# GLA hybrid trunk: the product for v with rows of h as TensorE's weights, and the decays moved one stage on

## The chip, the core and the metric

The program runs on one core of one Trainium2 chip. The time is the device time of one execution in microseconds (us); the median of three runs is compared. The engines are TensorE (PE in the profile, with its weight loads as PEld), VectorE (DVE), ScalarE (ACT), GpSimd (POOL) and SyncE (SP), which issues every DMA.

## What is computed

One layer of a decoder trunk on x of 1024 rows by 1024 columns. Only the parts that the change touches are shown; v has 4 heads of 256 columns, q and k 4 heads of 128.

```python
h = rms_norm(x, norm_mix_g)
proj = einsum('bsd,dc->bsc', h, w_in)
(q, k, v, z_a, gk_low, cb, cc, xc, z_c, g_a, g_c) = split(proj)
gk = log_sigmoid(gk_low @ w_gk2 + b_gk) / 16          # the decays
o = gla_chunked(q, k, v, gk)                          # rows of v by head and chunk
y_a = (rms_norm(o, gla_norm_g) * silu(z_a)) @ w_branch_a
u = causal_dwconv(cc * xc, conv_w)
y_c = ((cb * u) * silu(z_c)) @ w_branch_c
merged = sigmoid(g_a + b_ga) * y_a + sigmoid(g_c + b_gc) * y_c
x = x + merged @ w_out                                # then the per-layer embedding and a last norm
```

## The kernel before

**Products.** Every large product of 1024 by 1024 by 256 columns is a `Cell` (L695). It uses a seven-product scheme (Strassen-Winograd): both operands are cut in quarters, seven sums of quarters are multiplied, and the results are added. One operand stays in SBUF for a whole stage (`hres[0]` to `hres[6]`, the seven sums of h, each 128 x 4 x 512), the other comes from DRAM as four `raw` quarters and goes through a ring of eight buffer pairs (`RING`, L26). Each value is split in a high part `hi` (ScalarE's copy to fp32r) and a rest `lo` (VectorE's subtraction), and each product of 128 rows is three matmuls (`mm3`, L591): hi by hi, hi by lo, lo by hi. A product of a Cell has 4 slices of 128 in depth, so 12 matmuls of 512 columns; a Cell has 84. The accumulators X, Y and V are PSUM banks in two sets of three (tags m0 to m5); between products ScalarE copies X into Y and keeps c12 and c22 aside, and VectorE adds them back.

**The result of a Cell** has output columns on the partitions and rows of x along the free dimension: the piece of W is TensorE's weight and h streams. That is what q, k and the gates want. v is needed the other way round in `attend` (rows on the partitions), so `v_cons` takes each 128 x 512 result, has TensorE transpose it in four blocks of 128 x 128 into the PSUM tag "o" (`flip`, L1029), splits it there and stores both parts into the DRAM tensor `vd`. There are 4 heads x 4 results, so 16 flips with 64 transposes.

**Stages** follow one another, each with a memory pool of its own that takes the place of the pool before it: prep0 (norm, the sums of h, first gate products), v, qk, conv (which begins with the four `za` Cells), att, and so on. A buffer of a new pool waits for every user of the old pool. `run_groups` (L807) asks for the loads of a Cell's steps up to 14 steps ahead and for its splits up to 7 ahead.

**Order.** The program is not run as written: `Flow` records every operation and `put_in_order` (L404) then simulates all engines with fixed costs and emits, at each moment, the ready operation with the earliest due time. The main matmuls keep their written order; transposes and the matmuls of woven parts ("side" operations) are put between them. Because one helper issues everything, all rows of the profile say L491.

**Decays.** The generator `decays` (L1045) is woven into the v stage: two groups of 16 matmuls into `lowp`, eight into `zp`, and for each of four steps an Exp and a Ln on 128 x 1024 on ScalarE and two scans on VectorE; the results are stored to the DRAM tensor `cd`. The qk stage loads them as `cq` and `ck`. `za_cons` (L1168) applies a Sigmoid to each of the 16 results of the za Cells.

**Weights.** `weights` (L1181), woven into the conv stage, loads W_out and the gate matrix in eight loads of 1 MB as `wt`, forms sums in 32 VectorE operations and stores them to `wtd`.

Of the kernel before, what the change touches and what calls it, by code (L numbers as in the profile page):

```python
# [9 lines left out]
F32 = mybir.dt.float32  # L10
# [6 lines left out]
P = 128  # L17
# [3 lines left out]
H = 4  # L21
# [481 lines left out]
def kernel(  # L503
# [303 lines left out]
    def run_groups(groups, more=(), ahead=6):  # L807


        todo = line_up(groups)  # L810
        seq = todo + line_up(more)
        for n, (c, k) in enumerate(todo):
            for reach, what in ((RING + ahead, Cell.load), (RING - 1, Cell.prep)):
                for cc, kk in seq[n:n + reach]:
                    if not cc.ready(kk):
                        break
                    what(cc, kk)
            c.run(k)

    ep = phase("ev")  # L820
# [13 lines left out]

    def rows(b):
        return slice(b * P, (b + 1) * P)


    def gate_cons(c, bias, dst):
# [30 lines left out]


    W = {}
    for n, name in enumerate([f"v{h}" for h in range(4)] + ["q0", "k0", "q1", "k1"] + [f"za{h}" for h in range(4)]
                             + [f"{m}{g}" for g in range(4) for m in ("cc", "xc", "zc", "cb")]
                             + [f"ga{c}" for c in range(4)] + [f"gc{c}" for c in range(4)]
                             + [f"yc{c}" for c in range(4)] + [f"ya{c}" for c in range(4)]):
        W[name] = [wc[n, i // 2][:, i % 2] for i in range(4)]
# [13 lines left out]
    with phase("prep0") as pool:  # L891
# [122 lines left out]
        step(6)  # L1014
        step(5)


    nc.vector.tensor_scalar(ggla, ggla, float(P) ** -0.5, None, op0=ALU.mult)

    with phase("v", [ph["prep0"]]) as qp:  # L1020
        def v_cons(h):
            def cons(i, j, src):
                if j == 1:
                    t = src
                else:
                    t = ev(f"vt{h}_{i}_{j}")
                    nc.scalar.copy(t, src)

                def flip():  # L1029
# [3 lines left out]
                    hi = qp.tile([P, 4, P], F32R, tag="vhi", name=f"vhi{h}_{i}_{j}", bufs=2)  # L1033
                    lo = qp.tile([P, 4, P], F32R, tag="vlo", name=f"vlo{h}_{i}_{j}", bufs=2)
                    split(hi, lo, pt)
                    js = slice(j * P, (j + 1) * P)
                    store(vd[h][i][:, :, 0, js], f(hi))
                    store(vd[h][i][:, :, 1, js], f(lo))
                    return
                    yield  # L1040

                weave(flip(), 2)
            return cons

        def decays():  # L1045

            smask = qp.tile([P, HALF], F32, name="smask")
            nc.gpsimd.memset(smask, 1.0)
            nc.gpsimd.memset(smask.rearrange("p (c t) -> p c t", t=CH)[:, :, 0:1], 0.0)
            graw = qp.tile([P, 8, 16], F32, name="graw")  # L1050
            load(graw, wgl)
            gdif = qp.tile([P, 4, 16], F32, name="gdif")
            tt(gdif, graw[:, 4:8, :], graw[:, 0:4, :], op=ALU.subtract)


            glw = qp.tile([P, 12, 4, 32], F32R, name="glw")
            for i in range(4):
                split(glw[:, 0:8, i, 0:16], glw[:, 0:8, i, 16:32], graw)
                split(glw[:, 8:12, i, 0:16], glw[:, 8:12, i, 16:32], gdif)
            g2raw = qp.tile([P, 512], F32, name="g2raw")  # L1060
            load(g2raw, wgk2)
            g2 = qp.tile([P, 512], F32R, name="g2")
            nc.scalar.copy(g2, g2raw)
            tt(g2[64:128], g2raw[64:128], f(g2[64:128]), op=ALU.subtract)
            yield 2
            for half in range(2):

                ops = ((0, 0), (4, 3)) if half == 0 else ((0, 1), (8, 6))
                lowp = pso.tile([P, 512], F32, tag="o", name=f"lowp{half}", bufs=2)
                n = 0  # L1070
                for g0, k in ops:
                    for kt in range(4):
                        gl = glw[:, g0 + kt, :, :].rearrange("p a b -> p (a b)")
                        for s in range(2):
                            mm(lowp, gl, hres[k][s][:, kt, :], start=n == 0, stop=n == 15)
                            n += 1
                low = qp.tile([P, 512], F32R, tag="low", name=f"low{half}")
                nc.scalar.copy(low, lowp)
                for a in (32, 96):
                    tt(low[a:a + 32], lowp[a:a + 32], f(low[a:a + 32]), op=ALU.subtract)  # L1080
                yield 2
                for hp in range(2):
                    t1 = qp.tile([P, 2, HALF], F32, tag="t1", name=f"t1_{half}{hp}")
                    c = qp.tile([P, 2, HALF], F32, tag="c4", name=f"c4_{half}{hp}")
                    for i in range(2):
                        h = 2 * hp + i
                        zp = pso.tile([P, 512], F32, tag="o", name=f"zp{half}_{h}", bufs=2)
                        cs = slice(h * P, (h + 1) * P)
                        mm(zp, g2[:, cs], low, start=True, stop=True)
                        act(t1[:, i, :], zp, AF.Abs, bias=bgk[:, h:h + 1])  # L1090
                        nc.vector.tensor_scalar(c[:, i, :], zp, bgk[:, h:h + 1], 0.0, op0=ALU.add, op1=ALU.min)
# [9 lines left out]
        vs = [Cell(f"v{h}", "B", W[f"v{h}"], hres, v_cons(h)) for h in range(4)]  # L1101
        vs[0].begin = lambda: weave(decays(), 1)
        qks = []
        for hp in range(2):
            qks.append(Cell(f"q{hp}", "B", W[f"q{hp}"], hres, None))
            qks.append(Cell(f"k{hp}", "B", W[f"k{hp}"], hres, None))
        run_groups(single(vs), single(qks[:2]))
        finish_woven()

    with phase("qk", [ph["v"]]) as qp:  # L1110
        ex = lambda o, i_, sg: act(o, i_, AF.Exp, scale=sg / 16.0)

        def get_c(h, i, what):
# [51 lines left out]
        for hp in range(2):  # L1165
            qks[2 * hp].cons, qks[2 * hp + 1].cons = q_cons(hp), k_cons(hp)

        def za_cons(h):  # L1168
            def cons(i, j, src):
                t = ev(f"sz{h}_{i}_{j}")  # L1170
                act(t, src, AF.Sigmoid)
                stt(t, src, ggla[:, j:j + 1], t, op0=ALU.mult, op1=ALU.mult)
                store(szd[h][i][:, :, j, :], t.rearrange("p (n t) -> p n t", t=P))
            return cons

        zas = [Cell(f"za{h}", "B", W[f"za{h}"], hres, za_cons(h)) for h in range(4)]
        run_groups(single(qks), single(zas[:2]))


    with phase("conv", [ph["qk"]]) as vp:  # L1180
# [16 lines left out]
                        store(wtd[w][n][:, kt, :], q)  # L1197
                    yield 4

        convs = []  # L1200
        for g in range(4):
            t, u = [], []

# [31 lines left out]
                tt(us, src, us, op=ALU.mult)  # L1235
                store(ud[i][k // 4][:, k % 4, :], us)

            for m, cons in (("cc", cc_cons), ("xc", xc_cons), ("zc", zc_cons), ("cb", cb_cons)):
                convs.append(Cell(f"{m}{g}", "B", W[f"{m}{g}"], hres, cons, begin=cc_begin if m == "cc" else None))
# [10 lines left out]
    def attend(hp, ap, every):  # L1250
# [12 lines left out]
        def fetch(it):  # L1263
# [349 lines left out]
def _lay_out(inp):  # L1613
# [8 lines left out]
    cells = [col(v, h) for h in range(4)]  # L1622
    for hp in range(2):
        cells += [col(q, hp), col(k, hp)]
    cells += [col(za, h) for h in range(4)]
# [11 lines left out]
    wb = np.stack([np.stack(quads(a[n][0])) for n in ("w_out", "w_ple_gate")])  # L1637
# [37 lines left out]
```

## Time and profile before

| | |
|---|---|
| median of 3 runs | 1112.67 us (1112.47 to 1112.83) |
| the profiled execution | 1112.79 us |
| its span, first to last instruction | 1110.7 us |
| PE busy | 1098.1 us (99%), 5113 matmuls and transposes |
| PEld / DVE / ACT / POOL busy | 82% / 78% / 52% / 5% |
| granted TensorE clock, mean | 0.998 |

The busy time of PE counts modelled ends of pipelined matmuls, so a busy PE need not be at its peak: the distance between the starts of two matmuls tells the pace. Idle time of an engine that isn't the bottleneck costs nothing by itself.

### The profile page before, as it was taken

The page shows a single profiled execution, that of the slowest core. Times are in us where ns is not written, and L with a number is a line of the kernel's source. Part 1 is how long each engine was busy: PE and PEld are TensorE (multiplying, and loading weights), DVE is VectorE, ACT ScalarE, POOL GpSimd, SP SyncE. Part 2 cuts the span into 40 slices and gives each one's busy share as a digit, 9 for nine tenths or more (in the row PEclk, how much of TensorE's full clock was granted, in tenths as well). Part 3 has the DMA queues.
Part 4 walks back from the last instruction along what each step waited for, and adds up shares of the span by engine and source line. Part 5 has one row for each costly group of instructions (what it writes and reads, how often), then busy time and mean ns, then how long its engine had stood idle before and what let it go on. Part 6 is the DMA issues. An engine that isn't in the chain of part 4 may idle for free. (4 is left out here: it accounts for less than half of the span.)

```text
span 1110.7 us, 15381 instructions
## 1 busy us (share of the span) xinstructions
PE 1098.1 (99%) x5113; PEld 914.2 (82%) x5113; DVE 867.0 (78%) x1391; ACT 581.6 (52%) x1082; POOL 60.5 (5%) x121
## 2 busy tenths in 40 slices
PE   9999999999999999999999999999999999999996
PEld 7888888888888888888888888888888887788885
DVE  6997786997885856757649587876999879879676
ACT  6766765554443433333333376765735444467554
POOL 0000000000000000000000022230000000102022
PEclk9999999999999999999999999999999999999999
DMA  9953467888991131221212699988595888788843
GB/s 319 314 170 102 143 207 232 272 247 272 327 349 66 48 104 47 69 84 51 102 48 67 214 296 334 319 288 295 206 313 172 302 260 284 277 271 290 304 175 140
DMA packets 155582, 232.65 MB, mean 209 GB/s; under 512 B 12400, under 2 KB 74096, under 8 KB 152432
## 3 DMA queue, kind: packets, MB, share of 16 engines
q1 hardware_dynamic: 155504, 231.69, 62.0%
q8 instruction: 40, 0.66, 0.3%
q14 instruction: 38, 0.31, 0.1%
HBM read 154.04 MB, written 77.59 MB: 209 GB/s over the span
## 5 line engine op out<-in xcount | busy, mean ns | idle before, releaser
L491 ACT ACTIVATE junk<-x 128x512 bf16<-128x512 f32 (+1 forms) x33 | 20.3, 617 | 21.2 <-DVE x L491 18.9
L491 POOL MEMSET t<- 128x2 f32 x8 | 0.8, 100 | 443.9 <-DVE u L491 270.9
L491 DVE TENSOR_TENSOR wt<-wt 128x512 f32<-128x512 f32 x32 | 21.7, 685 | 0.2
L491 POOL TENSOR_TENSOR or<-or,mhalf 128x1 f32<-128x1 f32 x32 | 20.4, 639 | 2.7
L491 DVE SCALAR_TENSOR_TENSOR u<-t,vec,u 128x1024 f32<-128x1024 f32 x16 | 20.4, 1277 | 0.0
L491 POOL TENSOR_SCALAR rg<-ms 128x1 f32<-128x1 f32 x8 | 5.9, 738 | 265.8 <-ACT junk L491 265.8
L491 ACT ACTIVATE og<-op,or 128x256 f32<-128x256 f32 x32 | 15.1, 473 | 9.9 <-POOL or L491 5.8
L491 DVE COPY_PREDICATED aT<-trim,X 128x128 f32<-128x128 int32 x32 | 9.7, 302 | 10.8 <-PE X L491 10.2
L491 ACT ACT_TABLE_LOAD x12 | 15.4, 1283 | 0.9 <-PEq L1664 0.7
L491 DVE TENSOR_TENSOR oT<-op,szl 128x256 f32<-128x256 f32 x32 | 13.5, 421 | 2.8 <-DMA od<-oT 1.5
L491 DVE TENSOR_TENSOR gr<-pt_g,vec 128x512 f32<-128x512 f32 x16 | 10.7, 685 | 6.2 <-PE pt_g L491 3.6
L491 POOL TENSOR_SCALAR or<-oms 128x1 f32<-128x1 f32 x32 | 8.8, 274 | 119.0 <-ACT junk L491 119.0
L491 PE MATMUL op<-vl,aTh 128*128 128x256 f32 x64 | 15.0, 316 | 0.0
L491 ACT CAST aTh<-aT 128x128 fp32r<-128x128 f32 x32 | 9.5, 298 | 10.5 <-DVE aT L491 9.1
L491 PE MATMUL op<-Sh,qkl 128*128 128x256 f32 x56 | 14.5, 281 | 0.0
L491 ACT ACTIVATE junk<-op 128x256 bf16<-128x256 f32 x32 | 12.3, 385 | 2.0 <-PE op L491 1.7
L491 PE MATMUL pe<-wpehi,pThi 128*128 128x512 f32 x32 | 13.2, 412 | 0.0
L491 DVE TENSOR_TENSOR vlo<-pt_v,vhi 128x512 fp32r<-128x512 f32 x16 | 10.6, 681 | 2.9 <-ACT vhi L491 2.9
L491 DVE TENSOR_TENSOR Sl<-S,Sh 128x256 fp32r<-128x256 f32 x28 | 11.8, 420 | 1.4 <-ACT Sh L491 1.1
L491 PE MATMUL pe<-wpelo,pThi 128*128 128x512 f32 x32 | 12.8, 399 | 0.0
L491 PE MATMUL pe<-wpehi,pTlo 128*128 128x512 f32 x32 | 12.7, 398 | 0.0
L491 PEld LDWEIGHTS X<-vl,keh 128*128 128x128 f32 x56 | 10.4, 188 | 2.3
(3236 smaller groups left out, 4182.0 us busy)
## 6 DMA issues: line engine op xcount, KB each, us to landing
qkl<-qkd SPq DMA_DIRECT2D x32, 320.0 KB, 5.3
wt<-in_wb_dram SPq DMA_DIRECT2D x8, 1024.0 KB, 7.0
wtd<-wt SPq DMA_DIRECT2D x32, 256.0 KB, 4.7
vl<-vd SPq DMA_DIRECT2D x32, 256.0 KB, 5.4
uq<-ud SPq DMA_DIRECT2D x5, 1024.0 KB, 5.6
oq<-od SPq DMA_DIRECT2D x5, 1024.0 KB, 6.2
hq<-in_xT_dram SPq DMA_DIRECT2D x8, 512.0 KB, 6.6
ped<-pe SPq DMA_DIRECT2D x16, 256.0 KB, 4.6
```

What stands on the lines that cost most here:

```text
L491: o.call(*[place(a) for a in o.args], **{k: place(a) for k, a in o.kw.items()})
```

## The change

v's product is no longer four Cells but one object of a new class `Rows`. It has the same seven products of quarters, but on whole quarters of W_v (512 columns), with h's sums as TensorE's weights in blocks of 128 rows (`rows(s)`) and W_v's sums streaming. For each of the seven sums, in the order 0, 3, 2, 4, 6, 1, 5, four row blocks are run in turn, each into a PSUM bank of its own, and each with 4 x 3 matmuls. The results have rows on the partitions, so they are split straight from PSUM (or from the VectorE sum) and stored. `vd` is laid out by pairs of heads. W_v moves from the array `wc` to a third entry of `wb`. The decays move from the v stage to a new stage "za", in which the four za Cells run before q and k; they stood at the start of the conv stage. The pool of qk now follows that of za.

```diff
-    vd = [[dram(f"vd{h}_{i}", NP, 2, DV) for i in range(2)] for h in range(H)]
+    vd = [[dram(f"vd{j}_{i}", NP, 2, 2, DV) for i in range(2)] for j in range(2)]
...
+    class Rows:
+        order = (0, 3, 2, 4, 6, 1, 5)
+        need = {0: (0,), 3: (3,), 2: (1, 0, 2), 4: (), 6: (3,), 1: (), 5: (2,)}
...
+            self.prods = [(k, kt) for k in self.order for kt in range(4)]
...
+        def load(self, u):
+            k, kt = u
+            for n in self.need[k]:
+                if u not in self.ring and (u, n) not in self.raw:
+                    t = self.raw[u, n] = bp.tile([P, 512], F32, tag="raw", name=f"vraw{k}{n}_{kt}", bufs=8)
+                    load(t, self.src[n][:, kt, :])
+
+        def prep(self, u):
...
+            if k == 2:
+                b12, b11, b22 = (self.raw.pop((u, n)) for n in self.need[2])
+                t1 = self.pool.tile([P, 512], F32, tag="vt1", name=f"vT1_{kt}", bufs=4)
+                t2 = bp.tile([P, 512], F32, tag="T", name=f"vT2_{kt}", bufs=4)
+                tt(t1, b12, b11, op=ALU.subtract)
+                tt(t2, b22, t1, op=ALU.subtract)
+                tt(b12, b22, b12, op=ALU.subtract)
+                self.sums[1, kt], self.sums[2, kt], self.sums[4, kt] = t1, t2, b12
+                t = t2
+            elif k in (4, 1):
+                t = self.sums[k, kt]
+            elif k == 6:
+                t = self.sums[2, kt]
+                tt(t, self.raw.pop((u, 3)), t, op=ALU.subtract)
+            else:
+                t = self.raw.pop((u, self.need[k][0]))
+            hi = bp.tile([P, 512], F32R, tag="whi", name=f"v{k}{kt}hi", bufs=RING)
+            lo = bp.tile([P, 512], F32R, tag="wlo", name=f"v{k}{kt}lo", bufs=RING)
+            split(hi, lo, t)
+            self.ring[u] = hi, lo
+
+        def copy(self, tag, name, s):
+            t = self.pool.tile([P, 512], F32, tag=tag, name=f"{name}_{s}", bufs=4)
+            nc.scalar.copy(t, self.acc[s])
+            return t
+
+        def run(self, u):
+            k, kt = u
+            if kt < 3:
+                return
+            ahi, alo = self.res[k]
+            for s in range(4):
+                first = k in (0, 2, 1)
+                if first:
+                    self.acc[s] = psm.tile([P, 512], F32, tag=f"m{self.at % 6}", name=f"vacc{k}_{s}")
+                    self.at += 1
+                acc = self.acc[s]
+                if k == 2:
+                    nc.scalar.copy(acc, self.seed[s])
+                for t in range(4):
+                    bhi, blo = self.ring[k, t]
+                    nc.side = False
+                    mm3(acc, ahi[:, t, rows(s)], alo[:, t, rows(s)], bhi, blo, t == 0 and k in (0, 1), t == 3)
+                    nc.side = True
...
+                if k == 0:
+                    self.seed[s] = self.copy("vs", "vs1", s)
+                elif k == 3:
+                    self.cons(0, 0, s, acc)
...
-    with phase("v", [ph["prep0"]]) as qp:
-        def v_cons(h):
...
-                    pt = pso.tile([P, 4, P], F32, tag="o", name=f"pt_v{h}_{i}_{j}", bufs=2)
-                    for s in range(4):
-                        transpose(pt[:, s, :], t[:, s * P:(s + 1) * P])
...
+    with phase("v", [ph["prep0"]]) as vp:
+        def v_cons(i, j, s, src):
+            hi = vp.tile([P, 2, DV], F32R, tag="vhi", name=f"vhi{i}{j}_{s}", bufs=2)
+            lo = vp.tile([P, 2, DV], F32R, tag="vlo", name=f"vlo{i}{j}_{s}", bufs=2)
+            split(hi, lo, src.rearrange("p (h d) -> p h d", h=2))
+            store(vd[j][i][:, s, :, 0, :], f(hi))
+            store(vd[j][i][:, s, :, 1, :], f(lo))
...
+        run_groups(single([vrows]), single(zas[:2]))
+        finish_woven()
+
+    with phase("za", [ph["v"]]) as qp:
         def decays():
...
-        vs[0].begin = lambda: weave(decays(), 1)
...
-        run_groups(single(vs), single(qks[:2]))
+        zas[0].begin = lambda: weave(decays(), 1)
+        run_groups(single(zas), single(qks[:2]))
         finish_woven()

-    with phase("qk", [ph["v"]]) as qp:
+    with phase("qk", [ph["za"]]) as qp:
...
-        run_groups(single(qks), single(zas[:2]))
+        run_groups(single(qks), single(convs[:2]))
...
-        run_groups(single(zas + convs), pairs(gas[:2]))
+        run_groups(single(convs), pairs(gas[:2]))
...
-            load(f(v), vd[h][pr // NP][:, pr % NP])
+            load(f(v), vd[h // 2][pr // NP][:, pr % NP, h % 2])
```

## Rows read from the trace of the kernel before

**Rows 1.** The head of the profile's page: span, busy time and share of each engine with its instructions, and the granted TensorE clock in 40 slices of the span, in tenths (9 is 90% or more).

```profile
span 1110.7 us, 15381 instructions
PE 1098.1 (99%) x5113; PEld 914.2 (82%) x5113; DVE 867.0 (78%) x1391; ACT 581.6 (52%) x1082; POOL 60.5 (5%) x121
PEclk9999999999999999999999999999999999999999
```

**Rows 2.** The waits of PE over the whole span: who waited for whom, us in total, times, longest; the two longest of five.

```profile
PE warm L491 <- DVE zero L491: 1.4, 1, 1.4
PE out0V L491 <- ACT out0hi L491: 0.7, 1, 0.7
...
```

**Rows 3.** Busy time by stretch: start and end, length, then for PE, PEld, DVE, ACT and POOL the busy us with the instructions, the granted clock, the DMA engines' busy share and GB/s. The stretches are the v stage, the four za Cells, and the first four Cells of the convolution.

```profile
76.30:171.00 94.70, 94.69 (x446) 77.18 (x446) 76.60 (x118) 63.23 (x102) 0.64 (x2) 1.00 0.50 156
245.90:322.10 76.20, 76.20 (x338) 63.09 (x337) 62.23 (x100) 34.69 (x59) 0.20 (x2) 1.00 0.91 304
322.10:398.30 76.20, 76.20 (x338) 63.12 (x337) 55.08 (x83) 28.22 (x49) 0.20 (x2) 1.00 0.32 111
```

**Rows 4.** The timeline of PE: start, duration, what. First two rows of the embedding's product, in which blocks of p (`pT`) are the weights and `wpe` streams (two matmuls between them are left out); then the first matmul of each of the first three products of v (eleven between two of them are left out).

```profile
18.00 0.39 PE L491 MATMUL pe<-wpehi,pThi 128*128 128x512 f32 x1
...
18.68 0.39 PE L491 MATMUL pe<-wpehi,pThi 128*128 128x512 f32 x1
...
76.34 0.39 PE L491 MATMUL v0X<-h0hi,v0hi 128*128 128x512 f32 x1
...
79.06 0.39 PE L491 MATMUL v0V<-h1hi,v0hi 128*128 128x512 f32 x1
...
81.78 0.39 PE L491 MATMUL v0Y<-h2hi,v0hi 128*128 128x512 f32 x1
```

**Rows 5.** The timeline of PE around three flips. Left out are, of these two places, six matmuls of v1X between 109.08 and 110.94, and four of q0X between 169.28 and 170.67.

```profile
109.08 0.64 PE L491 MATMUL pt_v<-ident,v0u 128*128 128x128 f32 x4
...
110.94 0.39 PE L491 MATMUL v1X<-h3hi,v1hi 128*128 128x512 f32 x1
...
169.06 0.39 PE L491 MATMUL q0X<-h0hi,q0hi 128*128 128x512 f32 x1
169.28 0.62 PE L491 MATMUL pt_v<-ident,v3u 128*128 128x128 f32 x4
...
170.67 0.60 PE L491 MATMUL pt_v<-ident,vt 128*128 128x128 f32 x4
171.02 0.48 PE L491 MATMUL q0X<-h0hi,q0lo 128*128 128x512 f32 x1
171.34 0.39 PE L491 MATMUL q0X<-h0hi,q0hi 128*128 128x512 f32 x1
```

**Rows 6.** The timeline of PE at the first group of the decays' matmuls: its first, and the first matmul behind its 16.

```profile
92.44 0.39 PE L491 MATMUL lowp<-h0hi,glw 128*128 128x512 f32 x1
...
96.18 0.40 PE L491 MATMUL v0V<-h5hi,v0lo 128*128 128x512 f32 x1
```

**Rows 7.** Busy time of the instructions that write or read `pt_v`, in the v stage: PE, PEld, DVE and ACT with their counts, clock, DMA.

```profile
76.30:171.00 94.70, 9.22 (x64) 7.37 (x64) 9.28 (x14) 8.37 (x15) 1.00 0.50 156
```

**Rows 8.** The timeline of DVE where prep0 ends: the last operation on a buffer of its pool (`hq`), and two successive 128 x 512 operations of the ring.

```profile
82.41 1.21 DVE L491 TENSOR_TENSOR h6lo<-hq,h6hi 128x1024 fp32r<-128x1024 f32 x1
...
84.85 0.69 DVE L491 TENSOR_TENSOR v1T<-v1raw,v1T 128x512 f32<-128x512 f32 x1
85.46 0.68 DVE L491 TENSOR_TENSOR v1T<-v1raw,v1raw 128x512 f32<-128x512 f32 x1
```

**Rows 9.** The loads of the first Cell of v: issue time in ns (min/median/max), first and last start, and the time from issue to landing.

```profile
L491 SPq DMA_DIRECT2D v0raw<-in_wc_dram x4: 327/365/1391, 43.1 to 50.3; - x4
...
DMA to landing us min/median/max: 4.2/5.2/5.6
```

**Rows 10.** The timeline of ACT: the copy of X into Y behind the first product of v, and the first table load of the decays with its neighbours.

```profile
79.26 0.57 ACT L491 COPY v0Y<-v0X 128x512 f32<-128x512 f32 x1 [1.45 <-PE v0X L491]
...
102.93 0.58 ACT L491 COPY v1Y<-v1X 128x512 f32<-128x512 f32 x1
103.53 1.28 ACT L491 ACT_TABLE_LOAD   x1
104.82 1.06 ACT L491 ACTIVATE t<-t 128x1024 f32<-128x1024 f32 x1
```

**Rows 11.** All table loads, from the costliest groups of the page: count, busy us, mean ns, idle time before.

```profile
L491 ACT ACT_TABLE_LOAD x12 | 15.4, 1283 | 0.9 <-PEq L1664 0.7
```

**Rows 12.** The timeline of SP's queue: the decays' first load, their last store, and the first loads of the qk stage.

```profile
81.15 0.42 SPq L491 DMA_DIRECT2D graw<-in_wgl_dram  x1
...
165.47 0.33 SPq L491 DMA_DIRECT2D cd<-c  x1
...
179.94 1.81 SPq L491 DMA_DIRECT2D cq<-cd  x4
```

**Rows 13.** The timeline of PE where q1 begins: the next use of the bank in which q0's X stood.

```profile
208.08 0.39 PE L491 MATMUL q1X<-h0hi,q1hi 128*128 128x512 f32 x1
```

**Rows 14.** The sums of the woven weights: ns min/median/max, first and last start.

```profile
L491 DVE TENSOR_TENSOR wt<-wt x32: 678/683/693, 265.3 to 330.5; 128x512 f32<-128x512 f32 x32
```

**Rows 15.** The timeline of PE in the v stage where the distance to the next start is largest without a side operation before it.

```profile
145.56 0.39 PE L491 MATMUL v2Y<-h6lo,v2hi 128*128 128x512 f32 x1
145.95 0.63 PE L491 MATMUL pt_v<-ident,vt 128*128 128x128 f32 x4
```

More of the change, by code (lines that the diff above doesn't have):

```diff
@@ L812, in run_groups @@
         for n, (c, k) in enumerate(todo):
-            for reach, what in ((RING + ahead, Cell.load), (RING - 1, Cell.prep)):
+            for reach, what in ((RING + ahead, "load"), (RING - 1, "prep")):
                 for cc, kk in seq[n:n + reach]:
@@ L816, in run_groups @@
                         break
-                    what(cc, kk)
+                    getattr(cc, what)(kk)
             c.run(k)
@@ L836, in rows, with __init__ @@
         return slice(b * P, (b + 1) * P)
+    class Rows:
+        order = (0, 3, 2, 4, 6, 1, 5)
+        need = {0: (0,), 3: (3,), 2: (1, 0, 2), 4: (), 6: (3,), 1: (), 5: (2,)}
+        def __init__(self, src, res, pool, cons):
+            self.src, self.res, self.pool, self.cons = src, res, pool, cons
+            self.prods = [(k, kt) for k in self.order for kt in range(4)]
+            self.raw, self.ring, self.sums = {}, {}, {}
+            self.ready = lambda k: True
+            self.acc, self.seed, self.c12, self.at = [None] * 4, [None] * 4, [None] * 4, 0
+        def load(self, u):
[5 more added lines that the diff above has]
+        def prep(self, u):
+            if u in self.ring:
+                return
+            self.load(u)
+            k, kt = u
[24 more added lines that the diff above has]
+        def run(self, u):
+            k, kt = u
+            if kt < 3:
+                return
+            ahi, alo = self.res[k]
[12 more added lines that the diff above has]
+                    nc.side = True
+                    if t % 2 == 1:
+                        tick()
+                if k == 0:
+                    self.seed[s] = self.copy("vs", "vs1", s)
+                elif k == 3:
+                    self.cons(0, 0, s, acc)
+                elif k == 2:
+                    self.c12[s] = self.copy("vc", "vc12", s)
+                elif k == 4:
+                    self.seed[s] = self.copy("vs", "vc22", s)
+                elif k == 6:
+                    self.cons(1, 0, s, acc)
+                elif k == 1:
+                    tt(self.seed[s], acc, self.seed[s], op=ALU.add)
+                    self.cons(1, 1, s, self.seed[s])
+                else:
+                    tt(self.c12[s], acc, self.c12[s], op=ALU.add)
+                    self.cons(0, 1, s, self.c12[s])
@@ L872 @@
     W = {}
-    for n, name in enumerate([f"v{h}" for h in range(4)] + ["q0", "k0", "q1", "k1"] + [f"za{h}" for h in range(4)]
+    for n, name in enumerate(["q0", "k0", "q1", "k1"] + [f"za{h}" for h in range(4)]
                              + [f"{m}{g}" for g in range(4) for m in ("cc", "xc", "zc", "cb")]
@@ L1015 @@
         step(5)
+    convs = [Cell(f"{m}{g}", "B", W[f"{m}{g}"], hres, None) for g in range(4) for m in ("cc", "xc", "zc", "cb")]
     nc.vector.tensor_scalar(ggla, ggla, float(P) ** -0.5, None, op0=ALU.mult)
-    with phase("v", [ph["prep0"]]) as qp:
-        def v_cons(h):
[L1022 to L1029, printed above, removed]
-                    pt = pso.tile([P, 4, P], F32, tag="o", name=f"pt_v{h}_{i}_{j}", bufs=2)
-                    for s in range(4):
-                        transpose(pt[:, s, :], t[:, s * P:(s + 1) * P])
[L1033 to L1043, printed above, removed]
+    with phase("v", [ph["prep0"]]) as vp:
[5 more added lines that the diff above has]
+            store(vd[j][i][:, s, :, 1, :], f(lo))
+        qks = []
+        for hp in range(2):
+            qks.append(Cell(f"q{hp}", "B", W[f"q{hp}"], hres, None))
+            qks.append(Cell(f"k{hp}", "B", W[f"k{hp}"], hres, None))
+        vrows = Rows([wb[2, n] for n in (0, 1, 2, 3)], hres, vp, v_cons)
+        zas = [Cell(f"za{h}", "B", W[f"za{h}"], hres, None) for h in range(4)]
+        run_groups(single([vrows]), single(zas[:2]))
+        finish_woven()
+    with phase("za", [ph["v"]]) as qp:
         def decays():
@@ L1099, in decays, with za_cons, cons @@
                     yield 4
-        vs = [Cell(f"v{h}", "B", W[f"v{h}"], hres, v_cons(h)) for h in range(4)]
-        vs[0].begin = lambda: weave(decays(), 1)
[L1103 to L1106, printed above, removed]
-        run_groups(single(vs), single(qks[:2]))
+        def za_cons(h):
+            def cons(i, j, src):
+                t = ev(f"sz{h}_{i}_{j}")
+                act(t, src, AF.Sigmoid)
+                stt(t, src, ggla[:, j:j + 1], t, op0=ALU.mult, op1=ALU.mult)
+                store(szd[h][i][:, :, j, :], t.rearrange("p (n t) -> p n t", t=P))
+            return cons
+        for h in range(4):
+            zas[h].cons = za_cons(h)
+        zas[0].begin = lambda: weave(decays(), 1)
+        run_groups(single(zas), single(qks[:2]))
         finish_woven()
-    with phase("qk", [ph["v"]]) as qp:
+    with phase("qk", [ph["za"]]) as qp:
         ex = lambda o, i_, sg: act(o, i_, AF.Exp, scale=sg / 16.0)
@@ L1166 @@
             qks[2 * hp].cons, qks[2 * hp + 1].cons = q_cons(hp), k_cons(hp)
[L1168 to L1176, printed above, removed]
-        run_groups(single(qks), single(zas[:2]))
+        run_groups(single(qks), single(convs[:2]))
     with phase("conv", [ph["qk"]]) as vp:
@@ L1198, in weights @@
                     yield 4
-        convs = []
         for g in range(4):
@@ L1236, in cb_cons @@
                 store(ud[i][k // 4][:, k % 4, :], us)
-            for m, cons in (("cc", cc_cons), ("xc", xc_cons), ("zc", zc_cons), ("cb", cb_cons)):
-                convs.append(Cell(f"{m}{g}", "B", W[f"{m}{g}"], hres, cons, begin=cc_begin if m == "cc" else None))
+            for n, cons in enumerate((cc_cons, xc_cons, zc_cons, cb_cons)):
+                convs[4 * g + n].cons = cons
+            convs[4 * g].begin = cc_begin
         gas, gcs = ([Cell(f"{m}{c}", "B", W[f"{m}{c}"], hres, gate_cons(c, bias, dst), prods=(1, 2, 4, 5, 6),
@@ L1621, in _lay_out @@
     col = lambda m, n: m[:, n * 256:n * 256 + 256]
-    cells = [col(v, h) for h in range(4)]
+    cells = []
     for hp in range(2):
@@ L1636, in _lay_out @@
     wc = np.stack([np.stack([np.stack(quads(m)[0:2], 1), np.stack(quads(m)[2:4], 1)]) for m in cells])
-    wb = np.stack([np.stack(quads(a[n][0])) for n in ("w_out", "w_ple_gate")])
+    wb = np.stack([np.stack(quads(a[n][0])) for n in ("w_out", "w_ple_gate")] + [np.stack(quads(v))])
     pcol = lambda t: t.reshape(-1, 128).T
```

## Prediction, before the result was known

> **What bounds the kernel now.** I read the head of the page first, then the waits of PE, then the busy times by stage, and last the timeline of PE. The head shows PE busy for 1098.1 of 1110.7 us, and the clock row shows the upper of TensorE's two levels, 2.4 GHz, in every slice [rows 1]. Busy alone does not prove a bound, since ends of matmuls are modelled. The waits of PE do: beyond the 1.4 us at the start, the longest is 0.7 us, in the out stage [rows 2]. In the v stage PE is busy for 94.69 of 94.70 us, while VectorE has 76.60 and ScalarE 63.23 [rows 3]. So here every instruction that PE issues adds its own time, and only that counts, as long as nothing new makes PE wait.
>
> The pace: twelve matmuls of 512 columns start between 76.34 and 79.06, and twelve more by 81.78 [rows 4]. That is 2.72 us per twelve, 0.2267 us each.
>
> **The main matmuls.** Four Cells had 4 x 7 x 12 = 336 matmuls. Rows has 7 sums x 4 row blocks x 12 = 336, again with 128 x 128 weights and 512 streaming columns. I take 0.2267 us for each on both sides, so no change. That the operands trade places I cost at nothing. The trace shows h only as the streaming side, but the nearest rows are the embedding's: there blocks of activations are the weights and W streams, and three matmuls go from 18.00 to 18.68, 0.227 each [rows 4].
>
> **The transposes.** 64 go [rows 7]. A flip is not only its four transposes: the matmul behind it is slow too. From 109.08 to 110.94 stand one flip and six matmuls [rows 5]: 1.86 - 6 x 0.2267 = 0.50 us. From 169.06 to 171.34 stand two flips and six matmuls: 2.28 - 1.36 = 0.92, so 0.46 each. Sixteen flips give 7.4 to 8.0 us. A check over the whole stage: from 76.34 [rows 4] to 171.34 [rows 5] are 95.00 us, and in them 336 matmuls of v, 40 of the decays (16 and 16 into lowp, 8 into zp) and 6 of q0. 382 x 0.2267 = 86.60, so 8.40 us are left for flips and for what the decays cost over the pace. One group of 16 decay matmuls takes 96.18 - 92.44 = 3.74 [rows 6] against 3.63, so two cost 0.2 extra; zp and the matmuls behind them I put at as much or twice as much again. Then 7.8 us are the flips'. One stall of PE sits in it: 145.56 to 145.95 is 0.39, 0.17 above the pace [rows 15], and may not come back. **I take 7.7 us off, between 7.4 and 8.4** (all that is left over, if the decays mix better elsewhere).
>
> **The other work of v.** The ring needs 28 splits and 16 sums before and after. ScalarE had per Cell three copies of accumulators, two of results and four splits, 36 in all; now 16 copies and 16 splits. VectorE has 16 subtractions and 8 additions both times. At 0.6 us per operation, ScalarE wins some 2 us and VectorE nothing; both lie beside PE, which has more to do. Stores are 32 of the same 256 KB. Loads of W_v become 28 of 256 KB instead of 16, because the third sum takes three quarters and later sums load two of them again; the DMA engines are at half of their time in this stage [rows 3], so 3 MB more I cost at nothing, if they land in time.
>
> **The entry of v.** This is where a wait can arise. PE used one ring entry in 2.72 us; now it needs four within the first 2.72, and then none for 8.2. More delicate: the copies `vs1` and the sums `vT1` live in the new pool, so they wait for prep0's last operation, which ends at 82.41 + 1.21 = 83.62 [rows 8]. The first sum runs from 76.34 to 76.34 + 48 x 0.2267 = 87.22, the second to 98.10. The four copies (0.57 us each, [rows 10]) must begin to be done by 87.22: 3.6 us of cover. The third sum needs its four entries between 98.10 and 100.14. They are 16 VectorE operations at 0.61 each (84.85 to 85.46, [rows 8]), 9.8 us, and beside them at most four `lo` of the second sum and three of its results: 4.2 us. 83.62 + 14.0 = 97.6, so 2.5 us of cover. Its 12 loads have only eight buffers; the last four wait for the first sums and take 4.2 to 5.6 us to land [rows 9], which ends near 84.5 + 5.6 = 90.1, in time. I cost the entry at nothing; without that cover PE waits for the remainder.
>
> **The decays, moved.** 40 matmuls on PE stay 40, with the same 0.2 to 0.6 us of disturbance. They start when v's last store has landed: v ends at 76.34 + 336 x 0.2267 = 152.5, with its split and a landing about 158. Now they take from 81.15 to 165.47, 84.3 us [rows 12], so they would end near 242. za with the decays ends on PE at 152.5 + 76.2 + 9.5 = 238.2, and q0's first result is there four products later, at 249.1. If `cd` is late, the result waits in its bank, which PE wants again only when q1 begins, 208.08 [rows 13] against 169.06 [rows 5], 39 us after q0's start and 28 after that result. So it costs nothing.
>
> What it adds is table loads. v had no function of its own; za has 16 Sigmoids among the four Exp and Ln pairs. ScalarE's load: 34.69 us for za alone [rows 3]; v's stage has 63.23, of which 64 splits and copies at za's mean (34.69 / 59 = 0.59) are 37.6, so the decays take 25.6. Together 60.3 of 85.7 us. One switch costs 1.29 us: load at 103.53, Exp at 104.82 [rows 10], mean 1.283 [rows 11]. If each Sigmoid forced one more, 16 x 1.29 = 20.6 and ScalarE is at 81, still under PE. A single block matters more: a load and an Exp are 2.34 us, and the copy of X into Y has 81.78 [rows 4] - 79.26 - 0.57 [rows 10] = 1.95 us of cover. So a badly timed block costs PE 0.4 us. The v stage has eight such blocks now and one stall of 0.17 [rows 15]. I take 0.1 us more, from 0 to 24 x 0.4 = 9.6 at the far end.
>
> The Trainium skill, "ScalarE: Activation LUTs", section "Table sets: the hidden batching unit", asks that functions be batched by set, which this change undoes; its section "What ACT_TABLE_LOAD costs" puts 1.28 us on the load and a drain of 1.38 us on top. By that 2.66 us a block would be an estimated 3.7 us and a hit 1.8, and hits on eight blocks would make the sum 1119. The trace does not bear the drain out: the copy ends at 103.51, the load begins at 103.53 and Exp at 104.82 [rows 10].
>
> **The conv stage.** The weights' 32 sums, 0.68 us each [rows 14], ran beside za and will run beside the first conv Cells: 55.08 + 21.8 = 76.9 us of VectorE in 76.2 [rows 3], at most, since some of them are in the 55.08 already. Their results are wanted stages later, so the order can stretch them; I cost nothing, at most the 0.7 us.
>
> **Sum.** 1112.8 - 7.7 + 0.1 = 1105.2 us for the profiled execution; the median of the runs lies 0.1 below that and I leave it.
>
> **Rivals.** (a) *Tables in za.* Sigmoids fall between Exp and Ln, and eight to ten blocks hit a tight copy: 3 to 4 us back, 1108 to 1109. For it: nothing groups the Sigmoids, they come every 2.7 us. Against: ScalarE's 60.3 of 85.7. Chance 0.12. (b) *The entry of v, slower.* If each quarter of the third sum gets its three loads only after the quarter before has given its buffers back, a round is 5.6 + 3 x 0.61 = 7.4 us, four are 29.6, and the sums end at 113.2, 13 us behind 100.14: 1112.8 - 7.7 + 13 = 1118. It decides from 9.9 us of wait on. Against it: eight buffers hold two and a half quarters at once. Chance 0.06; half-sized (1107 to 1112) another 0.06. (c) *It doesn't pay.* PE loses the transposes but another engine sets the pace: 1112.7. Against it: v's VectorE work is 68 operations, 41 us of 76. Chance 0.03. (d) *More than said*: 8.4 us off and a late wait gone too, 1103 to 1104. Chance 0.05. The forecast, 1104.2 to 1107, has 0.68.
>
> **Chances and range.** This kernel's runs can tell a change from none at about 0.2%, 2.2 us, so faster means below 1110.4. Faster: 0.68 + 0.12 + 0.05 and most of the half-sized (b), 0.90. Same: (c) and the rest of that, 0.05. Slower: (b), 0.05. The range reaches from all 8.4 us and a little of (d), 1104.0, to 2.8 us of new waits, 1108.0.
>
> **What would show it.** Right: no `pt_v`; the matmuls of `vacc` at 0.227 us without gaps from 76.3 to 152.5; za with the decays in 85 to 86 us; the same picture from q0 on, 7.7 us earlier; 14 to 20 table loads. Wrong: waits of PE on `v2` splits near 98 us, on `vs1` near 87, on ACT copies into `za` accumulators, or in xc0 of the conv stage; a pace other than 0.227 with h as the weights would sink the first step, at 3.4 us for each hundredth.

## The result and the profile after

The changed kernel takes 1106.9 us in the median of five runs (1105.2 to 1108.74), the kernel before 1112.83 beside it (1112.47 to 1114.49): a ratio of 0.994, with the 95% interval 0.9929 to 0.9951. The profiled execution took 1105.2 us, as forecast; the median lies 1.7 above it, inside the range. How much of that agreement is earned, and how much is luck, is what the experiments are about.

The head of the page after, against [rows 1]: span, and busy time, share and instructions of each engine.

```profile
span 1103.1 us, 15242 instructions
...
PE 1090.3 (99%) x5049; PEld 907.2 (82%) x5049; DVE 864.9 (78%) x1391; ACT 588.2 (53%) x1083; POOL 60.9 (6%) x121
```

PE has 64 instructions fewer and 7.8 us less work; it is still the bound. Its longest waits in the whole execution, against [rows 2], are as before:

```profile
PE warm L491 <- DVE zero L491: 1.4, 1, 1.4
PE out0V L491 <- ACT out0hi L491: 0.7, 1, 0.7
PE out0V L491 <- DVE x L491: 0.4, 1, 0.4
```

The timeline of PE after, at the first matmul of v, of za and of the conv stage, against [rows 4]:

```profile
75.89 0.39 PE L491 MATMUL vacc<-v00hi,h0hi 128*128 128x512 f32 x1
...
152.05 0.39 PE L491 MATMUL za0X<-h0hi,za0hi 128*128 128x512 f32 x1
...
314.87 0.39 PE L491 MATMUL cc0X<-h0hi,cc0hi 128*128 128x512 f32 x1
```

The v stage lasts 152.05 - 75.89 = 76.16 us, and 336 x 0.2267 is 76.17: no gap at all. Busy time by stage says the same, against [rows 3]. The three stretches are v, za with the decays, and the first conv Cells; the columns are the length, PE, PEld, DVE, ACT and POOL with their instructions, the granted clock, the share of the DMA engines, and GB/s:

```profile
75.90:152.00 76.10, 76.10 (x337) 63.05 (x336) 48.11 (x76) 35.14 (x60) 0.64 (x2) 1.00 0.58 190
152.00:238.70 86.70, 86.56 (x377) 70.34 (x377) 68.86 (x109) 63.97 (x97) 0.00 (x0) 1.00 0.42 129
314.90:391.00 76.10, 76.10 (x337) 63.04 (x336) 62.78 (x99) 30.46 (x52) 0.40 (x4) 1.00 0.64 224
```

**One stretch for the accounting.** From the first matmul of v to the first of the conv stage's `cc0`, both kernels do the same work in another order: v, za, q and k (twelve Cells' worth, 1008 matmuls, 228.5 us at the pace) and the 40 matmuls of the decays (9.1 us). What a kernel takes beyond these 237.55 us is the price of transposes, mixing and waits. Before, the stretch starts at 76.34 [rows 4] and ends here:

```profile
322.32 0.39 PE L491 MATMUL cc0X<-h0hi,cc0hi 128*128 128x512 f32 x1
```

So before took 245.98 us, 8.43 beyond, and after 314.87 - 75.89 = 238.98, 1.43 beyond: 7.00 us gained. The rest of the 7.67 us between the two spans is small and lies outside: v starts 0.45 earlier, the stretch from `cc0` to the out stage is 0.04 shorter (615.57 for 615.61), and from there to the end 0.18 (172.62 for 172.80).

### The profile page after: what moved, and what is told of

Read it like the earlier page. It is cut to its first block, busy times and chain, and to the rows that moved or that the text cites. A ratio compares the mean times of both kernels' runs of the same rounds, so it can differ in the third digit from the quotient of the medians.

```text
span 1103.1 us, 15242 instructions
## 1 busy us (share of the span) xinstructions
PE 1090.3 (99%) x5049; PEld 907.2 (82%) x5049; DVE 864.9 (78%) x1391; ACT 588.2 (53%) x1083; POOL 60.9 (6%) x121
## 5 line engine op out<-in xcount | busy, mean ns | idle before, releaser
L491 PE MATMUL X<-qkl 128*128 128x128 f32 x64 | 12.3, 274 | 0.0
```

Source lines behind the costliest of these rows:

```text
L491: o.call(*[place(a) for a in o.args], **{k: place(a) for k, a in o.kw.items()})
```

## The experiments

Each profiled run gives a number of this stretch:

| kernel | v starts | cc0 starts | stretch | beyond 237.55 |
|---|---|---|---|---|
| before | 76.34 | 322.32 | 245.98 | 8.43 |
| after | 75.89 | 314.87 | 238.98 | 1.43 |
| after again (e1) | 76.30 | 315.71 | 239.41 | 1.86 |
| before without flips (e2) | 76.09 | 314.75 | 238.66 | 1.11 |
| before, decays moved (e3) | 75.56 | 322.23 | 246.67 | 9.12 |
| after, copies for Sigmoids (e4) | 76.01 | 314.75 | 238.74 | 1.19 |
| before, each flip twice (e9) | 76.02 | 328.76 | 252.74 | 15.19 |
| after beside (e10) | 76.19 | 315.19 | 239.00 | 1.45 |
| after, halved loads (e5) | 75.68 | 314.69 | 239.01 | 1.46 |
| after, halved loads (e11) | 75.98 | 314.99 | 239.01 | 1.46 |
| before, halved loads (e6) | 75.96 | 321.93 | 245.97 | 8.42 |

The halved loads of e5, e6 and e11 stand behind the stretch. So it repeats to 0.03 us from one execution to another, unless a wait comes in that the others have not, as in e1 (0.43, below). Differences of a few tenths between two kernels are to be read with that in mind.

**Before without its transposes (e2).** `v_cons` splits the result as it stands.

```diff
-                    pt = pso.tile([P, 4, P], F32, tag="o", name=f"pt_v{h}_{i}_{j}", bufs=2)
-                    for s in range(4):
-                        transpose(pt[:, s, :], t[:, s * P:(s + 1) * P])
+                    pt = t.rearrange("p (s t) -> p s t", t=P)
```

> The kernel before with the 64 transposes of v left out: each result is split and stored as it comes, so v is stored the wrong way round; everything else, the decays in the v stage too, stays. Theory (each flip costs PE 0.46 to 0.50 us, and nothing else of the change gives time): 7.4 to 8.0 us faster, 1104.8 to 1105.4. Rival (part of the gain is from the decays' new place): 3 to 5 us faster only, 1108 to 1110.

Measured: 1105.82 us (1105.22 to 1111.5, six runs), ratio 0.9942 (0.9926 to 0.9959), 0.4 above what was expected. The timeline of PE, the first matmul of v and of cc0:

```profile
76.09 0.39 PE L491 MATMUL v0X<-h0hi,v0hi 128*128 128x512 f32 x1
...
314.75 0.39 PE L491 MATMUL cc0X<-h0hi,cc0hi 128*128 128x512 f32 x1
```

The stretch falls by 7.32 us. Without `Rows`, without moved decays, taking the transposes out gives the whole gain. What stays of before's 8.43 us, 1.11, is what e2 takes over the pace: the decays' matmuls mixed into v, and the late starts of PE among them. These are not all the same as in before (e2 has one at 120.47 which before lacks, and lacks the stall of [rows 15]), so the split into 7.32 and 1.11 holds to two or three tenths.

**Before with each flip done twice (e9).** The same question from the other side.

```diff
-                    for s in range(4):
-                        transpose(pt[:, s, :], t[:, s * P:(s + 1) * P])
+                    for s in range(8):
+                        transpose(pt[:, s % 4, :], t[:, s % 4 * P:(s % 4 + 1) * P])
```

> The kernel before with every transposition of v done twice (64 more, into the same place, so the result is the same). In its trace four transposes of one flip take 0.35 to 0.39 us from start to start, and the matmul behind a flip starts its successor 0.09 us late; v's stage lost 7.3 us when the 16 flips went. Theory (a flip's price is its transposes at 0.109 us each plus a fixed part for the switch): 64 x 0.109 = 7.0 us more, 1119.0 to 1120.5. Rival (a flip's price is mostly the switch between matmuls and transposes, or the wait for its result): 1 to 4 us more, 1114 to 1117.

Measured: 1121.66 us (1119.04 to 1124.24, four runs), ratio 1.0087 (1.0068 to 1.0106). The median lies above what was expected, the profiled execution, 1119.04, in it; the four runs spread over 5.2 us, so the stretch is the better measure. The timeline of PE:

```profile
76.02 0.39 PE L491 MATMUL v0X<-h0hi,v0hi 128*128 128x512 f32 x1
...
328.76 0.39 PE L491 MATMUL cc0X<-h0hi,cc0hi 128*128 128x512 f32 x1
```

64 more transposes lengthen the stretch by 252.74 - 245.98 = 6.76 us, 0.106 each. By that the 64 transposes themselves are 6.76 of the 7.32 us, and 0.56 is left for entering and leaving a flip, some 0.035 for each of 16. That small rest hangs on two differences of single profiles; that the transposes are most of the price does not.

**Before with the decays moved alone (e3).** v stays four Cells with their flips; decays and za go to a stage of their own.

```diff
-        vs[0].begin = lambda: weave(decays(), 1)
-        run_groups(single(vs), single(qks[:2]))
+        run_groups(single(vs), single(zas[:2]))
+        finish_woven()
+
+    with phase("za", [ph["v"]]) as qp:
...
+        zas[0].begin = lambda: weave(decays(), 1)
+        run_groups(single(zas), single(qks[:2]))
```

> The other part alone: v as four Cells with its flips as before, but the decays woven into a za stage ahead of q and k as in the changed kernel. Theory: the move gives nothing and costs the waits seen in the za stage of the changed kernel, some 0.8 us: 1112.8 to 1114, table loads 16 to 18 instead of 12. Rival (the move gives time): below 1111.5.

Measured: 1113.19 us (1112.69 to 1115.86, eleven runs), ratio 1.0004 (0.9995 to 1.0013): no difference in the time. The timeline of PE:

```profile
75.56 0.39 PE L491 MATMUL v0X<-h0hi,v0hi 128*128 128x512 f32 x1
...
322.23 0.39 PE L491 MATMUL cc0X<-h0hi,cc0hi 128*128 128x512 f32 x1
```

The stretch grows by 0.69 us. So flips alone are -7.32, the move alone +0.69, and both together -7.00; the sum of the two single edits is -6.63, and 0.37 us is better in their company. That is the size of one late start of PE; where it comes from was not tested.

**After with copies in place of za's Sigmoids (e4).** It leaves the Sigmoid out, and so its table loads.

```diff
-                act(t, src, AF.Sigmoid)
+                act(t, src, AF.Copy)
```

> The changed kernel with the 16 Sigmoids of za replaced by plain copies, so that z_a is squared there instead of being gated by its Sigmoid; no table has to be loaded for them. If the Sigmoids' table loads make the three waits of PE in the za stage (0.8 us together), they go: 12 table loads and 1104.3 at best. If the waits come from the decays' own Exp and Ln, each a block of 2.3 us on ScalarE with its load, they stay: 1105.2.

Measured: 1105.36 us (1104.72 to 1109.81, six runs), ratio 0.9939 (0.9924 to 0.9955); the profiled execution was a long one, 1108.82, for a reason outside the stretch (see e1). All table loads of three kernels (count, busy us, mean ns, idle time before): first after, then e3, then this one, against 12 in [rows 11]:

```profile
L491 ACT ACT_TABLE_LOAD x17 | 21.8, 1283 | 3.4 <-issue 2.4 <-PEq L1745 0.7
```

```profile
L491 ACT ACT_TABLE_LOAD x18 | 23.1, 1283 | 1.0 <-PEq L1671 0.7
```

```profile
L491 ACT ACT_TABLE_LOAD x12 | 15.4, 1283 | 3.3 <-issue 2.4 <-PEq L1745 0.7
```

The five loads more that Sigmoids force cost the stretch 0.24 us (238.98 to 238.74). In after's za stage PE's starts are late at three places: 178.07 to 178.46 before `zp`, 195.37 to 195.79 before `lowp`, and 210.37 to 210.87 before `za2Y`. In e4 the middle one is gone; the other two stay (0.38 and 0.50), so they belong to the decays themselves. At the first of them no table load and no Exp is involved: `zp` waits for `ACT t`, ScalarE's read of the `zp` before it, and the first load of the stage begins only later. The timelines of PEld and ACT in after:

```profile
178.45 0.19 PEld L491 LDWEIGHTS zp<-low,g 128*128 128x128 f32 x1 [0.41 <-ACT t L491]
```

```profile
177.71 0.69 ACT L491 ACTIVATE t<-zp,vec 128x512 f32<-128x512 f32 x1 [0.59 <-DVE c L491]
...
179.41 1.28 ACT L491 ACT_TABLE_LOAD   x1
```

The third is the "hit" that the prediction described, though on another copy than the one of X into Y. The timelines of ACT and PE in after:

```profile
207.99 1.28 ACT L491 ACT_TABLE_LOAD   x1
209.28 1.06 ACT L491 ACTIVATE t<-t 128x1024 f32<-128x1024 f32 x1
210.25 0.57 ACT L491 COPY za2u<-za2Y 128x512 f32<-128x512 f32 x1
```

```profile
210.37 0.39 PE L491 MATMUL za2X<-h3hi,za2lo 128*128 128x512 f32 x1
210.87 0.50 PE L491 MATMUL za2Y<-h4hi,za2hi 128*128 128x512 f32 x1
```

The copy that frees the bank of `za2Y` stood behind a load and an Exp, and ends at 210.82; PE starts 0.05 later. The distance is 0.50, 0.27 above the pace, and the matmul itself reads 0.50 instead of 0.39: some 0.4 us in all, the price set in the prediction. The next function begins 1.29 us after the load does, so here too no drain follows it; the Trainium skill ("ScalarE: Activation LUTs", "What ACT_TABLE_LOAD costs") puts 1.38 us of drain on top, which this trace does not show.

**VectorE work at the entry of v (e7, e8).** How far is the entry of v from making PE wait? 6 and 12 operations without effect on the values are put behind the gate work of prep0, on VectorE: 6.8 and 13.7 us.

```diff
+        for _ in range(6):
+            tt(q[2][:, 0:2, :], q[2][:, 0:2, :], q[2][:, 0:2, :], op=ALU.max)
```

> The changed kernel with six more VectorE operations of 128 x 1024 on a buffer of prep0's pool, behind the last sum of h (a maximum of the buffer with itself, so nothing changes but time): 6 x 1.14 = 6.8 us. In the changed kernel prep0's last operation ends at 78.5, and the second sum of v needs the first copy in the new pool at 86.8. Theory (cover of 8.3 us less one copy of 0.6): no wait, 1105.2 as its short executions. Rival (the entry is as tight as the prediction's 2.5 us on the third sum): 3 to 5 us of waits, 1108 to 1110.

Measured: 1106.88 us (1106.25 to 1110.62, five runs), ratio 0.9957 (0.9943 to 0.9971), nearly as the theory has it. The v stage takes 76.68 us (75.66 to 152.34), 0.52 more than in after, and PE starts late where the third sum's last `lo` comes in:

```profile
100.05 0.50 PE L491 MATMUL vacc<-v23lo,h2hi 128*128 128x512 f32 x1 [0.20 <-DVE v23lo L491]
```

> The same with twelve such operations, 13.7 us. Theory: 13.7 - 7.7 = 6.0 us of PE waiting at the start of the second sum, near 86.8, and none at the third, whose sums move by as much as PE does: 1111 to 1112. Rival (PE waits at both, the sums and splits of the third sum being late on their own): 9 us or more, above 1114.

Measured: 1114.06 us (1113.41 to 1115.69, ten runs), ratio 1.001 (1.0001 to 1.0019): the gain is gone. The amount is the rival's, but not for its reason. za begins at 160.47 instead of 152.05, 8.4 us later, and 6.1 of these are lost before v, whose first matmul starts at 82.03. The timeline of PE in e8 near the start, and for 22 to 28 us the busy time, the granted clock and the DMA engines, first in e8, then in after:

```profile
19.15 0.49 PE L491 MATMUL pe<-wpehi,pThi 128*128 128x512 f32 x1 [0.61 <-ACT pThi L491]
21.27 0.66 PE L491 MATMUL rt<-ident,rb 128*128 128x128 f32 x4 [1.62 <-DVE rb L491]
21.68 0.68 PE L491 MATMUL pe<-wpelo,pThi 128*128 128x512 f32 x1
23.01 0.80 PE L491 MATMUL pe<-wpehi,pTlo 128*128 128x512 f32 x1 [0.65 <-DVE pTlo L491]
...
24.03 0.63 PE L491 MATMUL pe<-wpelo,pThi 128*128 128x512 f32 x1
24.45 0.63 PE L491 MATMUL pe<-wpehi,pTlo 128*128 128x512 f32 x1
24.88 0.63 PE L491 MATMUL pe<-wpehi,pThi 128*128 128x512 f32 x1
```

```profile
22.00:28.00 6.00, 5.36 (x13) 0.50 0.74 264
```

```profile
22.00:28.00 6.00, 6.00 (x30) 1.00 0.93 308
```

PE stands idle three times, 2.88 us together, where after has no wait, and the granted clock falls to the lower level, 1.2 GHz: matmuls of 512 columns then start 0.43 us apart instead of 0.227. The other 3.2 us of the 6.1 fit what that costs by an estimate, half of the six to seven us at the lower level. All ten executions of e8 have a mean granted clock of 0.993 to 0.995, those of after 0.996 to 0.998. The added operations are not what PE waits for there: the first of them starts at 53.8 us. With them the planner put all of prep0 in another order (two splits `pTlo`, for one of which PE waits, start at 12.44 and 15.30 in after, and the same two from 22.27 on in e8).

The v stage itself adds 2.3 us, at the second sum and at the third. These are the rival's two places, with a quarter of its 9 us:

```profile
94.00 0.50 PE L491 MATMUL vacc<-v30lo,h3hi 128*128 128x512 f32 x1 [0.70 <-DVE v30lo L491]
...
108.21 0.50 PE L491 MATMUL vacc<-v23lo,h2hi 128*128 128x512 f32 x1 [0.65 <-DVE v23lo L491]
```

So e8's 8.4 us are not the price of a tight entry. What VectorE has free at the entry can still be estimated from both runs: 6.8 - 0.5 = 6.3 us in e7, and 13.7 - 6.1 - 2.3 = 5.3 in e8, where PE came 6.1 later. The timeline of DVE in after shows the same cover: prep0's last operations end at 76.21 + 2.35 = 78.56, the last split of the third sum, `v23lo`, at 93.40, and PE wants it near 99.9, 6.5 us later.

```profile
76.21 2.35 DVE L491 TENSOR_TENSOR h5lo<-hq,h5hi 128x1024 fp32r<-128x1024 f32 x2
...
92.72 0.68 DVE L491 TENSOR_TENSOR v23lo<-vT,v23hi 128x512 fp32r<-128x512 f32 x1
```

**After once more (e1).** The kernel unchanged, for its spread.

> The changed kernel itself once more, to see the spread of its executions. Its profiled execution took 1105.2 us; the other four of its five took 1105.25 to 1108.74, while those of the kernel before took 1112.47 to 1114.49. Theory: PE issues back to back, so an execution at 1105.2 is the rule and the rest is added by waits that an execution has and another has not; a profile of a longer one shows them in one or two places. Rival: the whole program runs at a slower pace in a longer execution, then every stage is longer by the same share (0.2%, that is 0.05 us per 19 us Cell).

Measured: 1108.51 us (1105.5 to 1110.69, six runs), ratio 0.9953 (0.9937 to 0.997). Its profiled execution took 1108.25, 3.05 us longer than that of after. The rival, a slower pace everywhere, is out: v takes 76.16 us here too (76.30 to 152.46). 0.4 of it is at the start and 0.4 in one late start of the qk stage. Some 1.9 lie in the out stage, where ScalarE waits for a load of 1 MB (a quarter of the gate matrix) and PE for what follows from it, and 0.3 in a late start behind that. The waits of ACT between 990 and 1010 us, first in after, then in e1, and the wait of PE in e1:

```profile
ACT wg2hi L491 <- DMA wgq<-wtd: 0.9, 1, 0.9
```

```profile
ACT wg2hi L491 <- DMA wgq<-wtd: 3.0, 1, 3.0
...
PE out2Y L491 <- DVE x L491: 1.4, 1, 1.4
```

The four loads from `wtd` land after 4.8 to 8.3 us in after, after 4.9 to 10.3 in e1. e4's long profile shows the same place again, with other quarters:

```profile
ACT wg6hi L491 <- DMA wgq<-wtd: 3.1, 1, 3.1
...
ACT wg5hi L491 <- DMA wgq<-in_wb_dram: 1.6, 1, 1.6
```

From the first matmul of the out stage to the end it takes 176.4 us, e1 174.8, after and e10 172.6; from `cc0` to the out stage all four agree within 0.02. The order of instructions of ACT, DVE, SP and POOL from the out stage on is the same before and after the change, so the change did not make this wait.

**These loads in two halves, in after and in before (e5, e6).**

```diff
-            load(t, src[n])
+            for c in range(2):
+                load(t[:, 2 * c:2 * c + 2, :], src[n][:, 2 * c:2 * c + 2, :])
```

> The changed kernel with each 1 MB load of a quarter in the late stages (u, o, W_out, the gate matrix) issued as two loads of 512 KB, so that ScalarE's split of the first half can start when that half has landed. Theory (the longer executions come from gate-matrix quarters that land late in the out stage, where ScalarE stood idle 3.0 us for one of them in the longer execution and 0.9 in the short one): the short executions stay or gain up to 2 us, 1103 to 1105.5, and the spread of the six falls from 5 us to 2 or less. Rival (the spread is of the whole program, or of the memory and not of these loads): the same 1105 to 1110.

Measured: 1105.28 us (1104.45 to 1107.6, five runs), ratio 0.9933 (0.9921 to 0.9946); no wait of ACT on `wgq` is left in its profile, but in that of e11, the same kernel, there are two (1.0 and 0.5 us).

> The same halved loads in the kernel before. Theory: 1110.5 to 1113, with less spread, and the distance to the changed kernel with halves is what the turned product is worth by itself, 7.0 us from the v stage to the end of za and qk. Rival (the spread has another source and the halves do nothing): 1112 to 1114.5 as before.

Measured: 1112.02 us (1110.98 to 1112.5, eleven runs), ratio 0.9992 (0.9983 to 1.0001). On one chip and with halves on both sides the medians are 6.7 us apart (e5 and e6), where 7.0 were expected. Since e5 ran on another chip than e1, the two were put side by side on one, after (e10) and after with halves (e11).

> The changed kernel beside its version with halved loads, on one chip. Theory (late gate-matrix quarters make the longer executions): 1105.2 to 1110, median above 1106.

Measured: 1106.42 us (1105.47 to 1108.17, five runs), ratio 0.9947 (0.9933 to 0.9961).

> The changed kernel with halved loads, on the same chip as the one without. Theory: 1104.5 to 1106, median at least 1 us below the one without, and the longest execution below 1108. Rival (the spread does not hang on these loads and the narrower spread of the first run was luck): the same median and spread as the one without.

Measured: 1106.02 us (1104.51 to 1106.77, five runs), ratio 0.9938 (0.9925 to 0.9951). 0.4 us between medians and overlapping intervals: this does not tell the two apart. The longest execution is 1.4 us shorter with halves, which points the way of the theory and proves nothing. So the late loads are shown as the place of most of the loss in the two long profiles, e1 and e4, but that they account for after's spread is not shown.

## Why the prediction was right, and where it was not

**The bound.** Right. PE sets the time of the stretch in every kernel above, and what was taken from PE came off the end.

**The main matmuls.** Right: 76.16 us for 336 matmuls, the pace of 0.2267 with h as weights and W_v streaming.

**The transposes.** 7.7 us were taken off, between 7.4 and 8.4. They are worth 7.32 (e2), just under the lower bound. The step that was mis-sized is the division of what the stage has over the pace. The total was read well, 8.40 for a measured 8.43; but the decays' part was put at 0.6, and e2 has 1.11. Of that 0.6 only the 0.2 of the two `lowp` groups came from rows, and the share of `zp` was a guess. The flips themselves were priced well: the two near 169 gave 0.46 each, and the whole stage gives 7.32 / 16 = 0.46, of which 0.42 are the four transposes; the one near 109, at 0.50, lies above that mean.

**The entry of v.** Right that it costs nothing, with too small a cover: 2.5 us forecast, 5.3 to 6.5 found. The step took prep0's last operation to end at 83.62, as before [rows 8]; in after it ends at 78.56. From 58 us on eleven splits and sums of v's first Cell stood among prep0's operations; now four splits of `Rows` do. The rival of a chained entry (b) did not occur; even with 13.7 us more of VectorE's work ahead of v, PE waits only 2.3 us there (e8).

**The decays, moved.** `cd` was forecast to be stored near 242, without cost. SP's queue in after, against [rows 12]:

```profile
237.21 2.65 SPq L491 DMA_DIRECT2D cd<-c  x2
...
243.38 2.31 SPq L491 DMA_DIRECT2D cq<-cd  x4
```

The store ends its issue at 239.9, and no wait of PE stands behind it. What the move does cost is in PE's own stage. Table loads were put at 0.1 us; Sigmoids' loads cost 0.24 (e4), with 17 loads in all, inside the 14 to 20 named. za with the decays takes 238.71 - 152.05 = 86.66 us, a little over the 85 to 86 forecast: 1.43 beyond the pace, of which 0.62 are the three late starts (0.16, 0.19 and 0.27 over the pace) and some 0.3 in all the slow matmuls behind them. Against before the move is worse by 0.69 alone (e3) and by 0.32 in company (7.32 - 7.00), not by 0.1. Rival (a), 3 to 4 us of hits because Sigmoids fall between Exp and Ln, did not come: eight to ten hits on a copy were needed, one of 0.4 occurred, and it stays when the Sigmoids are gone (e4). The late start that does go with them, before `lowp`, is 0.3 with the slow matmul behind it.

**The conv stage.** Right: 62.78 us of VectorE in 76.1, below the 76.9 allowed, and the stretch from `cc0` to the out stage is the same to 0.04 us.

**The sum.** 7.6 us were forecast; the change itself gives 7.00 in the profiled pair. The transposes were put 0.4 too high and the move 0.2 too low. The other 0.6 us lie outside the stretch, most of them at v's start, which the table above has between 75.56 and 76.34 without regard to the change (75.89 and 76.30 for the same kernel). That the profiled execution came out at the forecast to the tenth is luck. And the medians beside each other differ by 5.9, not by 7.6. The prediction put the median 0.1 below its profiled execution, as before; that step failed too. The profiled execution of after was the shortest of its five, and all sixteen executions of the unchanged kernel have a median of about 1106.9. Why they spread over 5.5 us, where 17 of before on one chip stay within 2.6, is open; the late loads of e1 and e4 are a candidate.

## What to carry to other kernels

When the bound engine does a transpose only because a product comes out the wrong way round, turn the product: swap the stationary and the streaming operand, if the pace is the same both ways, and the transposes are simply gone. When the price of removed work is checked over a whole stage, read what stays there from rows as well: here a guess for it (0.6 for 1.11) was most of the error. When an experiment loads one engine, look at the granted clock and at where PE waits before the loss is read as that engine's: in e8 most of it was lost in another place. A forecast to the tenth of a microsecond of one execution says little when executions spread over 5 us: state the median's own range.

## What the runs showed of the hardware

- A 128 x 128 fp32 transpose between matmuls takes 0.106 us of PE's time (e9), and going from matmuls to transposes and back only some 0.035 per group of four. The list of instruction groups of before gives the mean of one as 273 ns (last number but one), since they overlap:

```profile
L491 PE MATMUL pt_v<-ident,vt 128*128 128x128 f32 x32 | 5.0, 273 | 0.0
```

- Loads of 1 MB in the same queue, with the same instructions around them, landed after at most 8.3 us in one execution and 10.3 in another; the tighter of the two waits behind them grew from 0.9 to 3.0 us.
- In e8 PE stood idle for 0.61, 1.62 and 0.65 us between 18.5 and 23.0; the granted clock was 0.90 from 21 to 22 us and 0.50, the lower of the two levels, from 22 to 28. The distance of matmuls of 512 columns went from 0.227 to 0.43 us. The idle time was 2.88 us, the loss at v's start 6.1.
